# Seven-product weight sums moved from VectorE to accumulating transfers on GpSimd's queue

## The chip, the cores and the metric

The kernel runs on one core of a Trainium2 chip. The metric is the device time of one launch, in microseconds. The core has TensorE (PE, matrix products), VectorE (DVE), ScalarE (ACT), GpSimd (POOL) and SyncE (SP). In this kernel every transfer before the change is issued from SP's queue.

## The reference

A decoder of two layers on 512 tokens of 1024 features, all float32. What matters here is the MLP that ends each layer:

```
def sq_relu_mlp(h, w1, w2):
    return jnp.square(jax.nn.relu(h @ w1)) @ w2      # h 512x1024, w1 1024x4096, w2 4096x1024
```

Layer 0 has a pooling mixer ahead of its MLP, layer 1 a spatial gating unit (SGU). Each layer's norms are modulated by vectors computed from `c` and `ada_w`.

## The kernel before

**Precision.** A float32 product is made of three matmuls of float32r operands (`mm3`, lines 123 to 127): each operand is split into a high part `h` and a remainder `l`. For weights `split` (lines 113 to 118) does that: ACT copies a 128x1024 piece to `wh` (L116), then DVE makes `wl = r - wh` (L117). The pairs `wh`, `wl` lie in five buffers, so a split waits until TensorE is done with the pair five splits earlier.

**The second MLP product** takes its 4096 inner features in four chunks `c` of 1024. Chunks 0 to 2 go by a seven-product scheme on 2x2 blocks (the p units). The last chunk is done plainly in eight q units. The weights of a chunk are four blocks of 1 MB each, named b11, b12, b21, b22 and loaded by `b_of` (L400) into three buffers `b`. The activations `g` are addressed through `quad`. Some products take sums of weight blocks and sums of activations:

- products 1, 3 and 2 take b11, b22 and b21 as they are loaded;
- products 5, 6 and 4 take one tile `t` that is carried on in place: product 5 makes it b12-b11 (L416), product 6 makes it b22-t (L422), product 4 makes it t-b21 (L441);
- product 7 takes b12-b22 (L433).

So VectorE makes four weight sums of 128x2048 in each of three chunks and two layers, 24 in all. Activation sums (L418, L424, L426, L430; tiles `s` and `u`) and the split of the activations into `oh` and `ol` (L445, L446) are there too.

**Units and order.** `mlp` (line 349) lists units: f units (one 128-wide piece of the first product, 24 matmuls, then ACT's relu and square, L374 and L375), p units (24 matmuls) and q units. In one chunk the order is f f f, then p1 f p5 f p6 f p3 f p7 f p2 p4, where p5 is the unit of product 5. TensorE's order is as written. `prep` of a unit (loads, sums, splits) is written two units ahead of its matmuls. The instructions of the other engines are put into an order by a scheduler when the kernel is built, and each engine then works through its own in that order. An engine whose next instruction has to wait holds back all that stands behind it.

**Results of a p unit** are added to a tile `y` in SBUF by VectorE (L474), or copied by ACT where it is the first (L477).

**Beside it**: `ada_tile` (L143 load, L147 multiply and sum on DVE) works off the modulation vectors during the MLP. `spread_cols` (lines 154 to 162) has eight GpSimd operations (`dg`, L158) that feed four matmuls `pb` (L161), which have a fixed place in TensorE's order. GpSimd does nothing else during the MLPs.

Of the kernel before, what the change touches and what calls it, by code (L numbers as in the profile page):

```python
# [7 lines left out]
F32 = mybir.dt.float32  # L8
F32R = mybir.dt.float32r
AF = mybir.ActivationFunctionType  # L10
ALU = mybir.AluOpType
# [3 lines left out]
P = 128  # L15
D = 1024
S = 512
KD = D // P
# [30 lines left out]
def decoder_kernel(ctx: ExitStack, tc: tile.TileContext, xtok, vecs, rows, fgrow, ada0, adag, ada1, pool_w, w1s, w1, w2, w2e, w_v, w_u, w_o, wsT, lnp, bs, out):  # L49
    nc = tc.nc  # L50
    V, A, G, T = nc.vector, nc.scalar, nc.gpsimd, nc.tensor
# [18 lines left out]
    def f32(t):  # L70
        return t.bitcast(F32)

    def bank(name, pool=None):
        pool = pool or ps
        return pool.tile([P, S], F32, name=name, tag="mm" if pool is ps else "xz")
# [26 lines left out]
    def raw4(src):  # L102
        r = w4.tile([P, D], F32, name="raw", tag="w4")
        nc.sync.dma_start(r, src)
        return r
# [4 lines left out]
    def wpair():  # L110
        return wtile("wh"), wtile("wl")

    def split(r):

        h, l = wpair()
        A.activation(h, r, AF.Copy)  # L116
        V.tensor_tensor(l, r, f32(h), ALU.subtract)  # L117
        return h, l

    def cut(hl_, *ix):  # L120
        return hl_[0][ix], hl_[1][ix]

    def mm3(o, w, m, first, last, **kw):
        (wh, wl), (mh, ml) = w, m
        T.matmul(o, wl, mh, start=first, stop=False, **kw)  # L125
        T.matmul(o, wh, ml, start=False, stop=False, **kw)  # L126
        T.matmul(o, wh, mh, start=False, stop=last, **kw)  # L127
# [37 lines left out]
    def rsqrt(src, mul, eps, n):  # L165
        v = sm.tile([P, n], F32, name="rv", tag=f"rv{n}")
        V.tensor_scalar(v, src, mul, eps, ALU.mult, ALU.add)  # L167
        r = sm.tile([P, n], F32, name="rr", tag=f"rr{n}")
        G.tensor_tensor(r, v, mhalf[:, 0:n], ALU.pow)  # L169
        t = sm.tile([P, n], F32, name="rt", tag=f"rt{n}")  # L170

        V.scalar_tensor_tensor(t, v, -0.5, r, ALU.mult, ALU.mult)
        V.tensor_tensor(t, t, r, ALU.mult)
        V.scalar_tensor_tensor(r, t, 1.5, r, ALU.add, ALU.mult)
        return r


    with tc.tile_pool(name="st", bufs=1) as st, tc.tile_pool(name="st2", bufs=2) as st2:
# [12 lines left out]
        for g in range(4):  # L191
# [4 lines left out]
            for n in range(2):  # L196
                m = pm[:, n]
# [151 lines left out]
    def mlp(i, first, extra, last, ending):  # L349
# [3 lines left out]
        with (  # L353
# [23 lines left out]
            def quad(c, r, j):  # L377

                return g[c, j].rearrange("p a (h r t) -> p a h r t", h=2, r=2)[:, :, :, r]
# [13 lines left out]

            held = {}

            def b_of(c, r, n):
                t = w2p.tile([P, 4, S], F32, name="b", tag="b")
                nc.sync.dma_start(t, w2[i, c, r, n])  # L400
                return t

            def p_prep(u):
                c, m = u
                H = held

                def s_tile(name):
                    return su.tile([P, 4, 2, P], F32, name=name, tag=name)

                if m == 1:  # L410
                    wb = H["b11"] = b_of(c, 0, 0)
                    a = quad(c, 0, 0)
                elif m == 5:
                    H["b12"] = b_of(c, 0, 1)
                    wb = H["t"] = H.pop("b11")
                    V.tensor_tensor(wb, H["b12"], wb, ALU.subtract)  # L416
                    a = H["s"] = s_tile("s")
                    V.tensor_tensor(a, quad(c, 1, 0), quad(c, 1, 1), ALU.add)  # L418
                elif m == 6:
                    H["b22"] = b_of(c, 1, 1)  # L420
                    wb = H["t"]
                    V.tensor_tensor(wb, H["b22"], wb, ALU.subtract)  # L422
                    a = H["s"]
                    V.tensor_tensor(a, a, quad(c, 0, 0), ALU.subtract)  # L424
                    H["u"] = s_tile("u")
                    V.tensor_tensor(H["u"], quad(c, 0, 0), quad(c, 1, 0), ALU.subtract)  # L426
                elif m == 3:
                    wb = H["b22"]
                    a = H["s"]
                    V.tensor_tensor(a, quad(c, 0, 1), a, ALU.subtract)  # L430
                elif m == 7:
                    wb = H.pop("b12")
                    V.tensor_tensor(wb, H.pop("b22"), wb, ALU.subtract)  # L433
                    a = H.pop("u")
                    H.pop("s")
                elif m == 2:
                    wb = H["b21"] = b_of(c, 1, 0)
                    a = quad(c, 0, 1)
                else:
                    wb = H.pop("t")  # L440
                    V.tensor_tensor(wb, H.pop("b21"), wb, ALU.subtract)  # L441
                    a = quad(c, 1, 1)
                oh = op.tile([P, 4, 2, P], F32R, name="oh", tag="oh")
                ol = op.tile([P, 4, 2, P], F32R, name="ol", tag="ol")
                A.activation(oh, a, AF.Copy)  # L445
                V.tensor_tensor(ol, a, f32(oh), ALU.subtract)  # L446
                w = [split(wb[:, 2 * q : 2 * q + 2].rearrange("p a b -> p (a b)")) for q in range(2)]
                return (oh, ol), w

            X, Z = {}, {}  # L450

            TAKES = {1: (0, 0), 5: (1, 1), 6: (0, 1), 3: (0, 1), 7: (1, 1), 2: (0, 0), 4: (1, 0)}
# [3 lines left out]
            def p_run(u, ready):  # L456
                halves = (0, 1)
                c, m = u
                o, w = ready
                banks = X if m in (1, 6, 7, 4) else Z  # L460
                first, fin = m in (1, 5, 2), m in (4, 3, 2)
                if first:
                    for hf in halves:
                        banks[hf] = bank("pm", xz)
                for p in range(4):
                    wv = cut(w[p // 2], ALL, slice(S * (p % 2), S * (p % 2) + S))
                    for hf in halves:
                        mm3(banks[hf], cut(o, ALL, p, hf), wv, first and p == 0, fin and p == 3, skip_group_check=True)
                for hf in halves:
                    r, dh = TAKES[m]  # L470
                    t = 2 * hf + r
                    yt = y[:, t, S * dh : S * dh + S]
                    if (t, dh) in seen:
                        V.tensor_tensor(yt, yt, banks[hf], ALU.add)  # L474
                    else:
                        seen.add((t, dh))
                        A.activation(yt, banks[hf], AF.Copy)  # L477
                    if c == 2 and LAST.get(m) == (r, dh):

                        V.tensor_tensor(yt, yt, gb[:, S * dh : S * dh + S], ALU.mult)  # L480
                        V.tensor_tensor(x[:, t, S * dh : S * dh + S], x[:, t, S * dh : S * dh + S], yt, ALU.add)
# [4 lines left out]
            def q_prep(u):  # L486
                dh, t = u
                if t == 0:
                    wq[dh] = [split(raw4(w2e[i, dh, q].rearrange("p a b -> p (a b)"))) for q in range(4)]
                if dh:  # L490
                    return kept[t]
                if t < 2:
                    oh = op.tile([P, KD, P], F32R, name="qh", tag="oh")
                    ol = op.tile([P, KD, P], F32R, name="ql", tag="ol")
                else:
                    o = w2p.tile([P, 2, KD, P], F32R, name="qo", tag="b")
                    oh, ol = o[:, 0], o[:, 1]
                for j in range(2):
                    a, k = g[3, j][:, :, tok[t]], slice(4 * j, 4 * j + 4)
                    A.activation(oh[:, k], a, AF.Copy)  # L500
                    V.tensor_tensor(ol[:, k], a, f32(oh[:, k]), ALU.subtract)
                kept[t] = oh, ol
                return kept[t]
# [14 lines left out]
            for c in range(3):  # L518
# [3 lines left out]
                for m in (1, 5, 6, 3, 7, 2, 4):  # L522
                    units.append(("p", (c, m)))
                    if fs:
                        units.append(fs.pop(0))
            units += [("q", (dh, t)) for dh in range(2) for t in range(NT)]
            prep = {"f": f_prep, "p": p_prep, "q": q_prep}
            run = {"f": f_run, "p": p_run, "q": q_run}
            ready = {}
            extra = list(extra)  # L530
# [57 lines left out]
    ex += [lambda: spread_cols(mods[0][:, c_g(1, 0) : c_g(1, 0) + KD])]  # L588
    ex += [lambda q=q: ada_tile(1, q, ada1[8 + q], get4) for q in range(24)]
    mlp(0, first0, ex, gated, lambda: normed(0, 1, 0))  # L590


# [6 lines left out]
    with (  # L599
# [8 lines left out]
        wb = vp.tile([P, 2, HEADS, P], F32, name="wsbs")  # L608
# [18 lines left out]
        for t in range(NT):  # L627
# [6 lines left out]
            r = rsqrt(ag[:, 1:2], 1.0, LN_EPS, 1)  # L634
# [73 lines left out]
    def last1(t, dh, yt):  # L708
        gated(t, dh, yt)
        if dh == 1:  # L710
            r = rms(t)
            for n in range(2):
                c = slice(S * n, S * n + S)
                V.scalar_tensor_tensor(x[:, t, c], x[:, t, c], r, fgb[0][:, c], ALU.mult, ALU.mult)
                nc.sync.dma_start(out[t, :, n], x[:, t, c])

    mlp(1, first1, ex, last1, lambda: None)


# [74 lines left out]
```

## Time and profile before

| | |
|---|---|
| time, median of 3 runs | 920.51 us (920.27 to 920.9) |
| the profiled execution's own time | 922.86 us |
| its span, first to last instruction | 921.1 us |
| PE busy | 96% of the span |
| DVE busy | 653.6 us, 71% |
| ACT busy | 418.3 us, 45% |
| POOL busy | 46.0 us, 5% |
| HBM read | 135.87 MB |
| transfers from SP's queue | 42.9% of 16 DMA engines' span |

The first MLP's units lie at about 121 to 410 us, the SGU at 410 to 562 us, the second MLP at 562 to 921 us. A busy TensorE is not one at its peak, because a matmul's modelled end overlaps the next one's start; so a stage is also read by the distance from one matmul's start to the next. A group's line reads: line, engine, operation, output <- inputs, count | busy us, mean ns of one | idle time of the engine just before, and what ended it.

### The profile page before, as it was taken

To read this page: it belongs to the slowest core of one execution; us is meant where nothing else is said; L and a number is where in the kernel's file an instruction comes from. 1 tells how busy PE (TensorE), PEld (TensorE's weight loads), DVE (VectorE), ACT (ScalarE), POOL (GpSimd) and SP (SyncE) were. 2 spreads that over 40 slices of the span, in tenths; PEclk is the share of its full clock that TensorE was granted. 3 is DMA by queue.
4 is the path that set the end of the run, shared out by engine and by line. 5 is a ranking of instruction groups with operands and counts; after the bars stand their busy time and mean duration, and the time that the engine had idled before them with its cause. 6 is when DMAs were issued, how large, how long until landed. Compare 5 with 4: busy or idle time off the path is not lost.

```text
span 921.1 us, 10624 instructions
## 1 busy us (share of the span) xinstructions
PE 884.2 (96%) x4054; PEld 729.7 (79%) x4054; DVE 653.6 (71%) x910; ACT 418.3 (45%) x592; POOL 46.0 (5%) x98
## 2 busy tenths in 40 slices
PE   5987999999999999999998898999999999999996
PEld 3975888788888888888877687988887888888875
DVE  3678787678888888757587836267677576667945
ACT  7262365554444455347222426265545445445421
POOL 5000002000000000000200000000004000000000
PEclk9997999999999999999999999999999999999998
DMA  9946762554455351513357504452443134112212
GB/s 359 409 142 224 268 246 92 182 191 152 155 188 176 122 181 49 204 67 138 116 171 240 183 23 158 162 184 69 158 139 122 39 122 168 54 51 87 92 46 92
DMA packets 35045, 138.67 MB, mean 151 GB/s; under 512 B 3889, under 2 KB 4017, under 8 KB 31665
## 3 DMA queue, kind: packets, MB, share of 16 engines
q1 hardware_dynamic: 34994, 137.99, 42.9%
q8 instruction: 32, 0.52, 0.2%
q14 instruction: 19, 0.16, 0.1%
HBM read 135.87 MB, written 2.10 MB: 150 GB/s over the span
## 4 chain that ended last, share of the span: by engine, by line
PE 83%; DVE 7%; DMA 4%; ACT 3%; issue 2%; POOL 1%; DVEq 0%; SPq 0%; POOLq 0%; ACTq 0%
PE po L125 15%; PE po L126 15%; PE po L127 15%; PE pm L126 11%; PE pm L127 11%; PE pm L125 11%; PE pg L263 2%; DVE wl L117 2%; DMA ada<-in_ada 1%; DVE ada L147 1%; ACT wh L116 1%; DMA raw<-in_w_u 1%; PE po L292 1%; PE pq L252 1%; DVE v L637 1%
## 5 line engine op out<-in xcount | busy, mean ns | idle before, releaser
L125 PE MATMUL po<-hh,wl 128*128 128x512 f32 (+1 forms) x608 | 233.8, 384 | 9.2 <-DVE wl L117 6.7
L126 PE MATMUL po<-hl,wh 128*128 128x512 f32 (+1 forms) x608 | 231.4, 381 | 0.9 <-DVE hl L329 0.9
L127 PE MATMUL po<-hh,wh 128*128 128x512 f32 (+1 forms) x608 | 231.2, 380 | 0.0
L117 DVE TENSOR_TENSOR wl<-raw,wh 128x1024 fp32r<-128x1024 f32 x97 | 118.4, 1222 | 53.4 <-ACT wh L116 53.3
L117 DVE TENSOR_TENSOR wl<-b,wh 128x1024 fp32r<-128x1024 f32 x84 | 102.5, 1221 | 68.2 <-ACT wh L116 68.2
L125 PEld LDWEIGHTS po<-hh,wl 128*128 128x128 f32 x608 | 115.7, 190 | 34.3 <-DVE wl L117 8.4
L116 ACT ACTIVATE wh<-raw 128x1024 fp32r<-128x1024 f32 x97 | 102.4, 1058 | 84.9 <-PE pm L127 33.8
L126 PEld LDWEIGHTS po<-hl,wh 128*128 128x128 f32 x608 | 115.7, 190 | 23.4 <-DVE hl L329 1.4
L127 PEld LDWEIGHTS po<-hh,wh 128*128 128x128 f32 x608 | 115.5, 190 | 21.4
L127 PE MATMUL pm<-wh,oh 128*128 128x512 f32 x336 | 130.7, 389 | 0.0
L125 PE MATMUL pm<-wh,ol 128*128 128x512 f32 x336 | 130.7, 389 | 0.0
L126 PE MATMUL pm<-wl,oh 128*128 128x512 f32 x336 | 130.7, 389 | 0.0
L374 ACT ACTIVATE g<-po 128x512 f32<-128x512 f32 x64 | 37.8, 599 | 165.3 <-PE po L127 165.3
L147 DVE SCALAR_TENSOR_TENSOR ada<-ada,cb 128x1024 f32<-128x1024 f32 x66 | 80.2, 1218 | 22.2 <-DMA ada<-in_ada 22.0
L116 ACT ACTIVATE wh<-b 128x1024 fp32r<-128x1024 f32 x84 | 88.4, 1052 | 15.2 <-PE pm L127 10.1
L126 PEld LDWEIGHTS pm<-wl,oh 128*128 128x128 f32 x336 | 63.0, 188 | 13.1
L127 PEld LDWEIGHTS pm<-wh,oh 128*128 128x128 f32 x336 | 63.1, 188 | 13.1
L125 PEld LDWEIGHTS pm<-wh,ol 128*128 128x128 f32 x336 | 63.1, 188 | 13.1
L551 ACT ACTIVATE tmp<-x 128x512 f32<-128x512 f32 x24 | 15.1, 630 | 71.5 <-DVE x L548 71.5
L474 DVE TENSOR_TENSOR y<-y,pm 128x512 f32<-128x512 f32 x68 | 43.4, 679 | 0.0
L375 ACT ACTIVATE g<-g 128x512 f32<-128x512 f32 x64 | 39.5, 627 | 0.0
L169 POOL TENSOR_TENSOR rr<-rv,mhalf 128x1 f32<-128x1 f32 (+1 forms) x18 | 12.8, 711 | 423.8 <-DVE rv L167 412.5
(145 smaller groups left out, 1145.0 us busy)
## 6 DMA issues: line engine op xcount, KB each, us to landing
ada<-in_ada SPq DMA_DIRECT2D x66, 512.0 KB, 4.2
raw<-in_w SPq DMA_DIRECT2D x57, 512.0 KB, 3.3
b<-in_w SPq DMA_DIRECT2D x24, 1024.0 KB, 4.8
raw<-in_w2e SPq DMA_DIRECT2D x16, 512.0 KB, 3.4
wh<-in_ada SPq DMA_DIRECT2D x11, 512.0 KB, 7.0
wl<-in_ada SPq DMA_DIRECT2D x11, 512.0 KB, 10.0
raw<-in_w_v SPq DMA_DIRECT2D x8, 512.0 KB, 3.8
raw<-in_w_u SPq DMA_DIRECT2D x8, 512.0 KB, 4.2
```

The source lines that it names most:

```text
L116: A.activation(h, r, AF.Copy)
L117: V.tensor_tensor(l, r, f32(h), ALU.subtract)
L125: T.matmul(o, wl, mh, start=first, stop=False, **kw)
L126: T.matmul(o, wh, ml, start=False, stop=False, **kw)
L127: T.matmul(o, wh, mh, start=False, stop=last, **kw)
L147: V.scalar_tensor_tensor(r, r, 1.0, cb, ALU.mult, ALU.mult, accum_out=pmv[i, b][:, j : j + 1])
L169: G.tensor_tensor(r, v, mhalf[:, 0:n], ALU.pow)
L263: T.matmul(o, cab[:, k], r[:, k], start=(k == 0), stop=False)
L374: A.activation(t, po, AF.Relu)
L375: A.activation(t, t, AF.Square)
L474: V.tensor_tensor(yt, yt, banks[hf], ALU.add)
L551: A.activation(tmp, x[:, t, c], AF.Square, accum_out=sums[t][:, dh : dh + 1])
```

## The change

The seven products are written in another form, in which all weight sums are additions: `t` is b11 for product 1, b11+b12 for product 5, b11+b12+b22 for product 6 and b11+b12+b22+b21 for product 4; product 7 takes b12+b22. The signs move to an activation sum (product 5 subtracts, product 3 adds) and to the results of products 6 and 7, which are subtracted from `y` or copied with a scale of -1.

The additions are made by transfers that read a weight block from HBM and add it to the tile in SBUF (`accum_op`), issued from GpSimd's queue as soon as the splits that read the tile's old contents are done. `t` has a tile of its own, `bt` with one buffer; `b` has two buffers in place of three. 24 DVE operations go; 24 transfers of 1 MB come. The plain loads stay 24.

```
 def b_of(c, r, n):
-    t = w2p.tile([P, 4, S], F32, name="b", tag="b")
+    t = w2p.tile([P, 4, S], F32, name="b", tag="b", bufs=2)
...
 if m == 1:
-    wb = H["b11"] = b_of(c, 0, 0)
+    wb = H["t"] = w2p.tile([P, 4, S], F32, name="bt", tag="bt", bufs=1)
+    nc.sync.dma_start(wb, w2[i, c, 0, 0])
 elif m == 5:
-    H["b12"] = b_of(c, 0, 1)
-    wb = H["t"] = H.pop("b11")
-    V.tensor_tensor(wb, H["b12"], wb, ALU.subtract)
+    wb = H["t"]
-    V.tensor_tensor(a, quad(c, 1, 0), quad(c, 1, 1), ALU.add)
+    V.tensor_tensor(a, quad(c, 1, 0), quad(c, 1, 1), ALU.subtract)
 elif m == 6:
-    H["b22"] = b_of(c, 1, 1)
     wb = H["t"]
-    V.tensor_tensor(wb, H["b22"], wb, ALU.subtract)
...
 elif m == 3:
-    wb = H["b22"]
-    V.tensor_tensor(a, quad(c, 0, 1), a, ALU.subtract)
+    wb = b_of(c, 1, 1)
+    H["b12"] = b_of(c, 0, 1)
+    V.tensor_tensor(a, quad(c, 0, 1), a, ALU.add)
 elif m == 7:
     wb = H.pop("b12")
-    V.tensor_tensor(wb, H.pop("b22"), wb, ALU.subtract)
 elif m == 2:
-    wb = H["b21"] = b_of(c, 1, 0)
+    wb = b_of(c, 1, 0)
 else:
     wb = H.pop("t")
-    V.tensor_tensor(wb, H.pop("b21"), wb, ALU.subtract)
...
 w = [split(wb[:, 2 * q : 2 * q + 2].rearrange("p a b -> p (a b)")) for q in range(2)]
+if m in NEXT:
+    G.dma_start(wb, w2[i, c, NEXT[m][0], NEXT[m][1]], accum_op=ALU.add)
+if m == 3:
+    G.dma_start(H["b12"], w2[i, c, 1, 1], accum_op=ALU.add)
...
+NEXT = {1: (0, 1), 5: (1, 1), 6: (1, 0)}
...
+minus = m in (6, 7)
-        V.tensor_tensor(yt, yt, banks[hf], ALU.add)
+        V.tensor_tensor(yt, yt, banks[hf], ALU.subtract if minus else ALU.add)
-        A.activation(yt, banks[hf], AF.Copy)
+        A.activation(yt, banks[hf], AF.Copy, scale=-1.0 if minus else 1.0)
```

More of the change, by code (lines that the diff above doesn't have):

```diff
@@ L427, in p_prep @@
                 elif m == 3:
-                    wb = H["b22"]
-                    a = H["s"]
-                    V.tensor_tensor(a, quad(c, 0, 1), a, ALU.subtract)
+                    wb = b_of(c, 1, 1)
+                    H["b12"] = b_of(c, 0, 1)
+                    a = H.pop("s")
+                    V.tensor_tensor(a, quad(c, 0, 1), a, ALU.add)
                 elif m == 7:
                     wb = H.pop("b12")
-                    V.tensor_tensor(wb, H.pop("b22"), wb, ALU.subtract)
                     a = H.pop("u")
-                    H.pop("s")
                 elif m == 2:
-                    wb = H["b21"] = b_of(c, 1, 0)
+                    wb = b_of(c, 1, 0)
                     a = quad(c, 0, 1)
@@ L468, in p_run @@
                         mm3(banks[hf], cut(o, ALL, p, hf), wv, first and p == 0, fin and p == 3, skip_group_check=True)
+                r, dh = TAKES[m]
+                minus = m in (6, 7)
                 for hf in halves:
-                    r, dh = TAKES[m]
                     t = 2 * hf + r
@@ L495, in q_prep @@
                 else:
-                    o = w2p.tile([P, 2, KD, P], F32R, name="qo", tag="b")
+                    o = w2p.tile([P, 2, KD, P], F32R, name="qo", tag="b", bufs=2)
                     oh, ol = o[:, 0], o[:, 1]
```

## The prediction

> **What bounds the kernel now.** I read the page's table of engines first, then busy time by stage, then who waited for whom, and last the order in time around one chunk.
>
> ```profile
> PE 884.2 (96%) x4054; PEld 729.7 (79%) x4054; DVE 653.6 (71%) x910; ACT 418.3 (45%) x592; POOL 46.0 (5%) x98
> ```
>
> Busy time by stage (columns: stretch, its length, then busy us of PE, PEld, DVE, ACT, POOL, granted clock, DMA share, GB/s); 121 to 366 is the first MLP's f and p units, 605 to 860 the second's:
>
> ```profile
> 121.00:366.00 245.00, 245.00 (x1079) 202.17 (x1078) 200.19 (x230) 123.48 (x154) 6.46 (x8) 1.00 0.45 152
> 562.00:605.00 43.00, 39.85 (x272) 36.87 (x271) 21.80 (x40) 23.14 (x38) 1.10 (x2) 0.96 0.46 171
> 605.00:860.00 255.00, 255.00 (x1122) 210.38 (x1123) 178.44 (x172) 126.61 (x159) 9.72 (x8) 1.00 0.31 108
> ```
>
> In both stretches that hold the changed work TensorE is never idle. Since a busy PE can hide slow issue, I checked the distance from one matmul's start to the next in the chain of waits there: 0.227 us, matmul after matmul, at clock 1.00. So a unit of 24 matmuls takes 5.44 us, and ScalarE's relu of successive f units starts at that distance too (212.68, 218.12, 223.56). VectorE is busy 82% (200.19 of 245) and 70% (178.44 of 255): it follows, it does not lead. PE's waits from 562 us on, which are for VectorE (total, times, longest):
>
> ```profile
> PE po L125 <- DVE wl L117: 3.1, 3, 1.7
> PE pm L126 <- DVE wl L117: 0.2, 1, 0.2
> ```
>
> The 3.1 us lie ahead of 605, in the start of the second MLP, where no weight sum stands. What the change frees is time of an engine on which TensorE does not wait.
>
> **The change part by part.** *Removed:* 24 sums on VectorE (groups by line; count, busy us, mean ns, idle before):
>
> ```profile
> L422 DVE TENSOR_TENSOR b<-b 128x2048 f32<-128x2048 f32 x6 | 13.7, 2287 | 0.1
> L416 DVE TENSOR_TENSOR b<-b 128x2048 f32<-128x2048 f32 x6 | 13.7, 2284 | 0.0
> L441 DVE TENSOR_TENSOR b<-b 128x2048 f32<-128x2048 f32 x6 | 13.7, 2283 | 0.0
> L433 DVE TENSOR_TENSOR b<-b 128x2048 f32<-128x2048 f32 x6 | 13.7, 2281 | 0.0
> ```
>
> 4 x 13.7 = 54.8 us of VectorE. All of it lies beside matmuls at full pace, so its worth in the span is 0. At most the two waits above could go, 3.3 us, if work of VectorE were pulled ahead; I take 0.
>
> *Kept:* signs change at no cost: the same operations on the same shapes. In the built order of the changed kernel TensorE, ScalarE and SP have the same operations in the same order as before (on SP some loads go to `bt`); VectorE's order lacks the 24 sums and is otherwise shuffled a little; GpSimd's has 24 transfers more, so the change does what it says.
>
> *Added:* 24 transfers of 1 MB that read HBM and add into SBUF. What they cost depends on one length: X, from the VectorE split that frees the tile to the landing of the sum. The trace has no such transfer and none from GpSimd's queue. Nearest rows, of plain 1 MB loads, the page's DMA part (count, KB, median us to landing) and the answer for tile `b`:
>
> ```profile
> b<-in_w SPq DMA_DIRECT2D x24, 1024.0 KB, 4.8
> ```
>
> ```profile
> DMA to landing us min/median/max: 4.6/4.8/8.1
> ```
>
> Below, X is at least a plain load's 4.6 us. Above, the slowest row is pool_w's 1 MB at the start, 11.7 us with the DMA engines at 0.77 share; if the add makes the bytes pass twice, 23.4 us. I take two median loads, 2 x 4.8 = 9.6 us, since the load of this very array is the nearest row and an add needs two operands fetched.
>
> The Trainium skill (Collectives: The Full Stack, The bandwidth ceiling) says that a transfer that adds has no cost for the add but needs two source reads, so that it ran at half the rate of a copy, about 31 GB/s per engine. By it 16 engines would need some 4.2 us for 1 MB, an estimate from that page, and X would be shorter than mine; no run here shows it yet, and the sum would be the same.
>
> *Is X hidden?* Tile `t` is a chain: split for p1, add, split for p5, add, split for p6. Chunk 1 of the first MLP, from the time order of VectorE and ScalarE (start, length, engine, line):
>
> ```profile
> 210.35 1.22 DVE L117 TENSOR_TENSOR wl<-b,wh 128x1024 fp32r<-128x1024 f32 x1
> ...
> 225.14 1.23 DVE L117 TENSOR_TENSOR wl<-b,wh 128x1024 fp32r<-128x1024 f32 x1 [2.20 <-ACT wh L116]
> ```
>
> ```profile
> 218.62 1.06 ACT L116 ACTIVATE wh<-b 128x1024 fp32r<-128x1024 f32 x1
> ...
> 224.06 1.05 ACT L116 ACTIVATE wh<-b 128x1024 fp32r<-128x1024 f32 x1
> ...
> 232.08 1.06 ACT L116 ACTIVATE wh<-b 128x1024 fp32r<-128x1024 f32 x1 [2.01 <-DVE b L422]
> ```
>
> ```profile
> 245.12 0.39 PE L125 MATMUL pm<-wh,ol 128*128 128x512 f32 x1
> ```
>
> p1's second split ends at 210.35 + 1.22 = 211.57; p5's are at 218.62 and 224.06 on ScalarE and end on VectorE at 226.4; p6's first is at 232.08; p6 starts on TensorE at 245.12. With X = 9.6 the first add lands at 221.2. ScalarE waits 2.6 us at 218.62, and the rest of p5's splits still ends about 226. The second add lands at 236.0, p6's split is done 1.05 + 1.23 us later, at 238.3: 6.8 us to spare. The third add (for p4, split at 269.8) and product 7's (b12 loaded from 188, used at 251.7) have over 15 us to spare.
>
> If X is longer, the chain moves as a whole: X, then 4.2 us (two wh of p5, two half-tile operations of ScalarE between them, one wl: 0.95 + 0.5 + 0.5 + 1.05 + 1.23), X again, then 2.3 us. It is late when 2X + 6.5 exceeds the time from p1's split to p6's start. That time, from the same rows of the six chunks, is 34.3, 33.55, 35.6, 35.1, 36.8 and 35.6 us. So the first chunk is late from X = 13.5 us, all from 15.2, and then the price is the sum of the six, 12X - 171 us, since p6 has to wait in TensorE's fixed order.
>
> *What is held up behind a waiting instruction:* on ScalarE the relu of an f unit and the next raw split. The latter is done some 10 us before use (split for f4 ends at 228.6, f4 starts at 239.4). On GpSimd, `dg` of the second MLP now stands behind an add; it ended at 704.9 and its matmuls `pb` started at 708.5, 3.6 us to spare; the add's tile is loaded by about 690, before `dg` could begin (695). On SP the `bt` load waits for p4's split just as a `b` load did (269.91 to 276.3). 24 MB more are read: four adds of two passes at the page's best rate, 409 GB/s, are 20.5 us of all engines per chunk of 81.8 us, so the DMA share would rise from 0.45 to about 0.70. That stays below the 0.77 of the start, and raw loads have 9 us of lead over a median landing of 3.3.
>
> **Sum:** 0 gained, 0 lost. The profiled execution took 922.86 us, 1.76 more than its span of 921.1 and 2.35 more than the median of the three runs. The same in the changed kernel gives a median of **920.5 us**.
>
> **Rivals.**
> - *The adds are late* (slower): place p6 in each chunk, price 2 us per us of X and chunk, deciding from X = 13.5. With two slowest plain landings, 2 x 8.1 = 16.2, 12 x 16.2 - 171 = 23 us: 943. At 23.4 us it is 110: 1030. For it: nothing shows how fast a transfer adds, and it now shares engines with raw and ada loads. Against: the median row leaves 3.9 us per add. Chance 0.26.
> - *GpSimd writes its transfers slowly beside a busy VectorE* (slightly slower). GpSimd's operations are stretched beside other work:
>
> ```profile
> L158 POOL TENSOR_SCALAR dg<-ident,mods x24: 597/602/2672, 156.2 to 704.3; 128x128 f32<-128x128 f32 x24
> ```
>
>   602 ns is the median; the longest, 2672, is in the stretch 695 to 705, where VectorE was busy 7.40 of 10 us (2.57 of 7 at 156 to 163, longest there 2389). If one add had to wait out four VectorE operations of 1.22 us, X would be 9.6 + 4.9 = 14.5 and the three shortest chunks would lose 1.2, 2.0 and 0.4 us: 924. The Trainium skill (SBUF — State Buffer, the box on "DVE blocks DMA") has such a rule: a transfer from GpSimd's queue is stalled while VectorE runs an operation that locks the shared port; but its part Who interferes with whom finds that for copies and not for tensor_tensor, which is nearly all of VectorE's work here, so I keep the chance small. Chance 0.13.
> - *VectorE's free time shortens a start-up* (faster): up to 3.3 us of waits, 918. Against: they stand where no sum was removed. Chance 0.07.
>
> Forecast 0.54. A change under 0.2% (1.84 us) can hardly be told from none. So faster 0.07, same 0.54, slower 0.39. The range runs from 918 to 945, which leaves out about half of the late-add rival and little else, some 0.13; the likeliest case alone is 918.7 to 922.3.
>
> **What would show it.** Right: VectorE near 600 us, TensorE without a wait between 121 and 366 and between 605 and 860, start distance 0.227 us, X below 13.5 us. Wrong: waits of ScalarE's `wh<-bt` for transfers that exceed 10 us, followed by waits of PE `pm` for `wl` ahead of p6; or `pb` waiting for `dg`. The forecast fails if X is over 13.5 us, or if plain loads land later than their 9 us of lead.

## The result and the profile after

The changed kernel takes **931.08 us** (median of 4 runs, 929.4 to 934.34), the kernel before 920.7 us beside it (median of 4, 920.27 to 921.37): a ratio of 1.0116, 95% interval 1.0088 to 1.0145, so it is **slower by 1.2%**. The profiled execution took 930.9 us with a span of 929.2 us, 8.1 us more than the span before, at nearly the same mean clock (0.988 against 0.986).

The page's table of engines, of the changed kernel:

```profile
PE 884.1 (95%) x4054; PEld 727.2 (78%) x4054; DVE 601.1 (65%) x886; ACT 415.2 (45%) x592; POOL 71.8 (8%) x122
```

VectorE lost 52.5 us of work (653.6 to 601.1), TensorE has as much as before, and the span grew: TensorE idles more. Where, is told by the busy time by stage (columns as above: stretch, length, then PE, PEld, DVE, ACT, POOL, granted clock, DMA share, GB/s):

```profile
121.00:366.00 245.00, 236.78 (x1033) 193.06 (x1032) 161.79 (x202) 112.46 (x143) 21.60 (x20) 1.00 0.69 201
562.00:605.00 43.00, 39.92 (x265) 36.73 (x264) 22.11 (x47) 20.03 (x31) 2.59 (x4) 0.96 0.57 195
605.00:860.00 255.00, 254.92 (x1130) 210.45 (x1129) 148.48 (x153) 128.28 (x163) 19.40 (x19) 1.00 0.55 153
```

All of the loss is in the first MLP, 8.2 us of TensorE idle in 245. The second, with the same twelve adding transfers, keeps TensorE busy for 254.92 of 255. The next stage confirms it: GpSimd's first operation of the norm between the MLP and the gating unit starts at 409.96 us in place of 400.63, 9.3 later. That is the 8.2 us, and 0.16 us for each of the seven waits listed below: idle time is counted from the modelled end of a matmul, 0.39 us after its start, where the next would have started after 0.227.

Who waited for whom between 121 and 366 us (total, times, longest):

```profile
DVE ada L147 <- DMA ada<-in_ada: 72.7, 23, 11.1
ACT wh L116 <- DMA bt<-in_w: 58.1, 7, 15.1
...
PE pm L126 <- DVE wl L117: 3.5, 4, 1.3
PE po L125 <- DVE wl L117: 3.2, 2, 2.0
PE pm L125 <- ACT wh L116: 1.5, 1, 1.5
```

The same query on the kernel before:

```profile
DVE ada L147 <- DMA ada<-in_ada: 5.3, 6, 1.7
```

Read this from the bottom. TensorE's three rows add up to 8.2 us, all of the idle time. They are waits for splits. ScalarE's splits wait for `bt`, the tile into which the transfers add. The first row shown is in no account of the change: VectorE's wait for its **ada** loads went from 5.3 to 72.7 us, though nothing in the diff touches them.

The DMA part gives the lengths (count, KB, median us to landing):

```profile
ada<-in_ada SPq DMA_DIRECT2D x66, 512.0 KB, 5.5
bt<-in_w POOLq DMA_DIRECT2D x18, 1024.0 KB, 8.7
b<-in_w POOLq DMA_DIRECT2D x6, 1024.0 KB, 10.7
```

An add into `bt` lands 8.7 us after its issue, so X is near the 9.6 us of the prediction. Half a megabyte of ada, within the first MLP alone, before and after (two answers on the tile `ada`):

```profile
DMA to landing us min/median/max: 3.1/3.5/5.5
```

```profile
DMA to landing us min/median/max: 3.1/6.1/12.1
```

How the two meet is seen in chunk 0, in the order in time of GpSimd, ScalarE, VectorE and TensorE of the changed kernel:

```profile
127.37 1.06 POOL L450 DMA_DIRECT2D bt<-in_w  x1 [59.69 <-DVE wl L117]
128.16 1.18 POOL L452 DMA_DIRECT2D b<-in_w  x1
151.84 0.86 POOL L450 DMA_DIRECT2D bt<-in_w  x1 [22.49 <-DVE wl L117]
```

```profile
135.52 1.06 ACT L116 ACTIVATE wh<-bt 128x1024 fp32r<-128x1024 f32 x1 [1.57 <-DMA bt<-in_w]
139.28 1.05 ACT L116 ACTIVATE wh<-bt 128x1024 fp32r<-128x1024 f32 x1
...
160.90 1.06 ACT L116 ACTIVATE wh<-bt 128x1024 fp32r<-128x1024 f32 x1 [15.12 <-DMA bt<-in_w]
```

```profile
144.67 1.23 DVE L147 SCALAR_TENSOR_TENSOR ada<-ada,cb 128x1024 f32<-128x1024 f32 x1 [11.05 <-DMA ada<-in_ada]
...
145.82 1.22 DVE L117 TENSOR_TENSOR wl<-bt,wh 128x1024 fp32r<-128x1024 f32 x1
...
149.18 1.23 DVE L147 SCALAR_TENSOR_TENSOR ada<-ada,cb 128x1024 f32<-128x1024 f32 x1 [2.06 <-DMA ada<-in_ada]
...
150.33 1.22 DVE L117 TENSOR_TENSOR wl<-bt,wh 128x1024 fp32r<-128x1024 f32 x1
```

```profile
162.01 0.49 PE L125 MATMUL pm<-wh,ol 128*128 128x512 f32 x1 [1.50 <-ACT wh L116]
```

The first add is issued at 127.37 and has landed at 135.52, when ScalarE starts p5's split on it. ScalarE is done with both halves at 140.33. VectorE's part of the split, though, comes at 145.82 and 150.33: VectorE takes its work in a fixed order, and ahead of it stand two multiplies on ada tiles. The first of these tiles was issued at 132.51, while the adds into `bt` and `b` (127.37 and 128.16) were in flight, and lands 12.1 us later. VectorE does nothing for 11.05 us with a split behind it whose input has been there since 136.6. So the second add leaves at 151.84, lands at 160.9, and p6 starts 1.5 us late. From the first add's landing to the second's issue it took 16.3 us, where the prediction had 4.2.

### The profile page after: what moved, and what is told of

Its sections match the earlier page's. It is cut to its first block, busy times and chain, and to the rows that moved or that the text cites. A ratio compares the mean times of both kernels' runs of the same rounds, so it can differ in the third digit from the quotient of the medians.

```text
span 929.2 us, 10693 instructions
## 1 busy us (share of the span) xinstructions
PE 884.1 (95%) x4054; PEld 727.2 (78%) x4054; DVE 601.1 (65%) x886; ACT 415.2 (45%) x592; POOL 71.8 (8%) x122
## 3 DMA queue, kind: packets, MB, share of 16 engines
q0 software_dynamic: 3456, 25.17, 14.7%
## 4 chain that ended last, share of the span: by engine, by line
PE 60%; DMA 20%; DVE 11%; issue 4%; ACT 3%; POOL 1%; DVEq 0%; SPq 0%; POOLq 0%; ACTq 0%
DMA ada<-in_ada 15%; PE po L125 10%; PE po L126 10%; PE po L127 10%; PE pm L126 8%; PE pm L127 8%; PE pm L125 8%; DVE wl L117 4%; DVE ada L147 2%; PE pg L263 2%; ACT wh L116 1%; DMA wh<-in_ada 1%; PE po L292 1%; DMA bt<-in_w 1%; DMA raw<-in_w_u 1%
## 5 line engine op out<-in xcount | busy, mean ns | idle before, releaser
L117 DVE TENSOR_TENSOR wl<-bt,wh 128x1024 fp32r<-128x1024 f32 x48 | 58.4, 1223 | 47.2 <-ACT wh L116 47.2
L116 ACT ACTIVATE wh<-bt 128x1024 fp32r<-128x1024 f32 x48 | 50.5, 1055 | 80.7 <-DMA bt<-in_w 75.7
L117 DVE TENSOR_TENSOR wl<-b,wh 128x1024 fp32r<-128x1024 f32 x36 | 43.9, 1221 | 16.5 <-ACT wh L116 16.4
L450 POOL DMA_DIRECT2D bt<-in_w x18 | 15.9, 886 | 329.8 <-DVE wl L117 317.7
```

Source lines behind the costliest of these rows:

```text
L450: G.dma_start(wb, w2[i, c, NEXT[m][0], NEXT[m][1]], accum_op=ALU.add)
```

## The experiments

Theory A: ada loads land late beside adding transfers, and VectorE, which takes them in its order, passes their lateness to the splits behind them. Theory B, the rival: two adding transfers in a row are by themselves too long for the time from p1's split to p6's start. All were run in five rounds beside the kernel before, whose median was 921.52, 921.07 and 920.94 us in the three groups (experiments 1 to 4, 5 to 8, 9 to 12). Experiments 6 and 11 edit the kernel before, the others the changed kernel.

**1. The new form with its sums on VectorE.** Of the change, the signs alone.

```
-wb = H["t"]
+H["b12"] = b_of(c, 0, 1)
+wb = H["t"] = H.pop("b11")
+V.tensor_tensor(wb, H["b12"], wb, ALU.add)
...
-if m in NEXT:
-    G.dma_start(wb, w2[i, c, NEXT[m][0], NEXT[m][1]], accum_op=ALU.add)
```

> The changed kernel's form of the seven products (all weight sums additions, signs in an activation sum and in the results) with the 24 sums made by VectorE again and three b buffers, no transfer that adds. Both theories put the loss on the transfers and give the time before: 920.7 us, within 0.2%. If the signs or the order of products cost something, it shows here: then up to 931.

Measured 921.66 us, ratio 1.0001 (0.9992 to 1.0011); TensorE busy 245 of 245 us. The form costs nothing; the transfers are the cause.

**2 and 3. Adding transfers in one MLP only**: `add = i == 1` in the second, `add = i == 0` in the first, with the other MLP as in experiment 1.

> Adding transfers in the second MLP only, VectorE's sums (in the new form) in the first. Theory A (loads of ada tiles land late beside the adding transfers, and VectorE, which waits for them in its order, holds back the splits; ada tiles are many in the first MLP only) gives the time before, 920.7 us within 0.2%. Theory B (two adding transfers one after the other are by themselves too long for the time between p1's split and p6) gives about half of the loss, 925 to 926, since three of the six chunks are here.

> Adding transfers in the first MLP only. Theory A gives the whole loss, 929 to 932 us. Theory B gives half of it, 925 to 926.

In the second MLP alone: 921.24 us, ratio 0.9998 (0.999 to 1.0007), with an add landing in 8.7 us all the same. In the first alone: 937.6 us, ratio 1.0178 (1.0154 to 1.0201), VectorE's wait for ada there 75.1 us. So an add of this length is hidden where few ada tiles stand (8 in the second MLP, 32 in the first), and the first MLP holds all of the loss. That experiment 3 lost more than the whole change was not expected; experiments 9 and 10 return to it.

**4. The same transfers as plain copies.** Without `accum_op`, the sums are left out; queue, size, order and waits stay.

```
-G.dma_start(wb, w2[i, c, NEXT[m][0], NEXT[m][1]], accum_op=ALU.add)
+G.dma_start(wb, w2[i, c, NEXT[m][0], NEXT[m][1]])
```

> As the changed kernel, but the 24 transfers from GpSimd's queue are plain copies that overwrite the tile (the weight sums are left out). If an adding transfer passes its bytes twice, a plain one takes about half of the DMA engines' time (queue share 7% to 8% in place of 14.7%) and lands in 5 to 6 us in place of 8.6. Theory A: ada loads land sooner, VectorE waits for them less than half as long in the first MLP (under 35 us in place of 72.7), the time is 921 to 924. Theory B: the chain is 2 x 3 us shorter per chunk, the waits of p6 go, the time is 921 to 923 too; the two differ in whether VectorE's wait for ada goes with it.

Measured 921.51 us, ratio 0.9999 (0.999 to 1.0008). The DMA rows of the page, first the changed kernel's queue of adds, then this one's (packets, MB, share of 16 engines; then count, KB, us to landing):

```profile
q0 software_dynamic: 3456, 25.17, 14.7%
```

```profile
q0 software_dynamic: 3456, 25.17, 7.7%
...
bt<-in_w POOLq DMA_DIRECT2D x18, 1024.0 KB, 5.1
```

The same packets and bytes take the engines 14.7 x 929.2 / (7.7 x 919.8) = 1.9 times as long as an add. As copies they land in 5.1 us and ada in 4.4 (6.1 beside adds), and VectorE's wait for ada is 36.4 us in 22 waits of at most 3.5: a little over the 35 that theory A had set, and too short to matter. The two `b` buffers and the tile `bt` are as in the changed kernel. So it is the add, with its longer time on the DMA engines, that hurts, and not the buffers, GpSimd's queue or its waits. Both theories expect that.

**5 and 6. The changed kernel, and the kernel before, without the 32 ada tiles of the first MLP** (what they compute is filled with a constant).

```
-ex = [lambda q=q: ada_tile(0, 40 + q, ada1[q], get4) for q in range(8)]
+ex = [lambda: None for q in range(8)]
```

> The changed kernel without the 32 ada tiles of the first MLP (neither loaded nor multiplied; the modulation vectors that they give are filled with 0.5). Theory A: no wait is left for TensorE in the first MLP, the same time as the kernel before without these tiles, within 0.2%. Theory B: p6 still waits in the first MLP, 3 to 5 us more than that kernel.

> The kernel before without the 32 ada tiles of the first MLP (neither loaded nor multiplied; the modulation vectors that they give are filled with 0.5). TensorE was never idle there, so both theories give the time before or very little less: 919 to 921 us. It is the base for the changed kernel without these tiles.

Measured 921.36 us, ratio 1.0002 (0.9993 to 1.0011), and 921.17 us, 0.9998 (0.9986 to 1.0009). The adds still land in 8.6 us, and TensorE has no wait left. **Theory B falls**: two adds in a row fit into the time that they have.

**7. The 32 ada multiplies kept, their loads left out**: VectorE multiplies the tile `cb` in place of a loaded one.

> The changed kernel with the 32 ada tiles of the first MLP multiplied but not loaded: VectorE has the same operations, on the tile cb in place of a loaded one (so the modulation vectors differ). Theory A (the late landing is what holds VectorE back): no wait is left, 920 to 922 us. If it is VectorE's work on ada, or its new order, and not the landing: 928 to 931. Theory B: p6 still waits, 923 to 926.

Measured 920.73 us, ratio 0.9992 (0.998 to 1.0003). It is not VectorE's time on the ada tiles but the wait for their loads. Nor did the other transfers land sooner for want of the ada loads: the adds into `bt` take 8.4 us and the raw loads 4.6, against 8.7 and 4.3 in the changed kernel.

**8. Each add into `t` cut into two of 512 KB**, each issued when its own half has been split.

```
-G.dma_start(wb, w2[i, c, NEXT[m][0], NEXT[m][1]], accum_op=ALU.add)
+for q in range(2):
+    G.dma_start(wb[:, 2 * q : 2 * q + 2],
+                w2[i, c, NEXT[m][0], NEXT[m][1]][:, 2 * q : 2 * q + 2], accum_op=ALU.add)
```

> The changed kernel with each adding transfer into t cut into two halves of 512 KB, each issued when its own half has been split; the same bytes. Theory B: the chain from p1's split to p6 is some 4 to 8 us shorter per chunk, the waits of p6 (4.4 of the 8.2 us) go, 925 to 927 us or less. Theory A: the bytes and the landing of ada tiles are as before, so VectorE is still held back; the waits of f units (3.3 us) and part of p6's stay, 927 to 931.

Measured 920.99 us, ratio 0.9996 (0.9985 to 1.0008). **Theory A's expectation missed**: the late ada loads are all there, and yet the loss is gone, with the waits of the f units that A expected to stay. (B's "or less" was met, though experiment 5 rules B out.) The waits from 121 to 366 us, and the same place of chunk 0, on VectorE, ScalarE and TensorE:

```profile
DVE ada L147 <- DMA ada<-in_ada: 66.3, 24, 11.2
ACT wh L116 <- DMA bt<-in_w: 41.2, 10, 6.3
```

```profile
144.20 1.23 DVE L147 SCALAR_TENSOR_TENSOR ada<-ada,cb 128x1024 f32<-128x1024 f32 x1 [11.20 <-DMA ada<-in_ada]
...
145.35 1.22 DVE L117 TENSOR_TENSOR wl<-bt,wh 128x1024 fp32r<-128x1024 f32 x1
```

```profile
152.55 1.06 ACT L116 ACTIVATE wh<-bt 128x1024 fp32r<-128x1024 f32 x1 [6.17 <-DMA bt<-in_w]
...
160.36 1.07 ACT L116 ACTIVATE wh<-bt 128x1024 fp32r<-128x1024 f32 x1 [6.27 <-DMA bt<-in_w]
```

```profile
160.95 0.39 PE L125 MATMUL pm<-wh,ol 128*128 128x512 f32 x1
```

VectorE stands still for ada as long as in the changed kernel (11.20 us, until 144.20). But the first half's add no longer waits for the second half's split, is there at 152.55, and p6, which begins on that half, starts at 160.95 without a wait. So the loss needs both: a late ada load ahead of p5's splits, and a chain whose every link waits for the whole tile. Take away either (5 and 7 the one, 8 the other) and it is gone. One thing beside the cut differs in number 8: VectorE's order as built has p6's first split ahead of an ada multiply in chunks 1 and 2 (in chunk 1 at 236.78, the multiply at 241.25), where the changed kernel has both splits behind it (the multiply at 245.96, the splits at 247.11). What the cut and the order each gave there was not told apart; in chunk 0 no ada multiply stands between p5's splits and p6's first one in either.

**9 and 10. The changed kernel and experiment 3 once more, side by side**, unedited.

> The changed kernel as it is, beside the next run, to learn whether the larger loss with adds in the first MLP alone (937.6 against 931.1 us) belongs to that kernel or to the occasion. If to the occasion, this and the next one give medians within 2 us of each other; if to the kernel, this gives 929 to 934 and the next one 934 to 941 again. In both cases all idle time of TensorE in the two MLPs lies in the first one: TensorE busy 234 to 238 of 245 us between 121 and 366 us, VectorE's wait for ada loads there 65 to 80 us.

> Adding transfers in the first MLP alone, sums of the second on VectorE. Occasion: within 2 us of the changed kernel of the same call. Kernel: 934 to 941 us, 4 us and more above it.

Measured 935.35 us, ratio 1.0168 (1.015 to 1.0186), and 934.16 us, 1.0144 (1.013 to 1.0158): 1.2 us apart. The larger loss of experiment 3 belonged to the occasion and not to the kernel. TensorE is busy 236.31 of 245 us in number 9, as expected, and 239.10 in number 10, more than the 238 expected; VectorE waits for ada 71.3 and 73.4 us. So neither TensorE's idle time nor the lateness of ada tells why these runs are slower than those of the first comparison: number 10 idles 2.3 us less there than the changed kernel's first profile, and its profiled execution took 3.2 us more (934.07 against 930.9). What differs is the granted clock. Two stretches of number 9, each at the start of a p6 (columns as above, the clock behind POOL):

```profile
163.23:170.06 6.83, 6.23 (x15) 4.94 (x16) 6.78 (x9) 6.83 (x10) 3.43 (x2) 0.50 0.49 113
337.31:340.72 3.41, 3.05 (x7) 2.47 (x8) 2.41 (x3) 3.41 (x5) 0.88 (x1) 0.50 0.49 154
```

At half clock the matmuls start 0.427 us apart in place of 0.227, so these 10.2 us lose some 4.8 (an estimate: 10.2 x (1 - 0.227/0.427)); number 9's profiled execution was 4.1 us slower than the first. Number 10 has 10.2 us of the same, at the starts of two p6, and experiment 3 has 6.8. The first profile has none: there the clock is 1.00 at the same place, behind waits of 1.50 and 0.76 us against 1.58 and 0.76 in number 9. What decides whether the clock drops behind such a wait stays open. The loss is 1.2 to 1.8% over these four comparisons. Kernels without the loss do not vary so (experiments 1, 2 and 4 to 8 lie within 1 us of each other), and none of their profiles has such a stretch in the first MLP.

**11 and 12. What VectorE's freed time is worth.** If VectorE has time to spare in the first MLP, it can take over the 16 ada tiles of the gating unit, whose loads head 9.6 us of VectorE's idle time between 440 and 526 us while TensorE idles 5.5. Number 11 moves them in the kernel before, with all its sums on VectorE; number 12 in the kernel of experiment 8.

```
-ex += [lambda q=q: ada_tile(1, q, ada1[8 + q], get4) for q in range(24)]
+ex += [lambda q=q: ada_tile(1, q, ada1[8 + q], get4) for q in range(40)]
...
-    ex += [lambda q=q: ada_tile(1, q, ada1[8 + q], get4) for q in range(24, 40)]
```

> The kernel before with the 16 ada tiles of the gating unit (440 to 526 us, where TensorE idles 5.5 of 86 us and VectorE is busy 68) moved into the first MLP, which then has 48 of them; no adding transfers. VectorE in 121 to 366 us goes from 200.2 to about 200.2 + 16 x 1.22 = 219.7 of 245 us. If what holds up TensorE in the gating unit is VectorE's order with its ada loads (they head 9.6 us of its idle time there), 3 to 5 us are gained: 916 to 918. If it is something else in the gating unit, 920.5 to 921.5. If the first MLP has no room for 16 more tiles, over 922.

> The same move of 16 ada tiles on top of the changed kernel with its adds into t cut into halves. VectorE in 121 to 366 us about 172.5 + 19.5 = 192 of 245 us. If VectorE's time is what the first MLP lacks for more ada tiles, this is the faster of the two moves (916 to 918). If it is the late ada loads beside adding transfers and the slack of the chain, as the runs so far say, 48 tiles in place of 32 bring the idle time of TensorE back, and this is slower than the move without adding transfers, by 2 to 10 us (920 to 928).

Number 11 measured **913.9 us, ratio 0.9922 (0.991 to 0.9935)**, faster than both kernels and than expected; number 12 938.02 us, 1.0187 (1.0169 to 1.0205), worse than the 920 to 928 expected. Busy time by stage, 11 and then 12:

```profile
121.00:366.00 245.00, 244.54 (x1075) 201.48 (x1075) 217.43 (x271) 125.52 (x158) 13.34 (x8) 1.00 0.53 183
440.00:526.00 86.00, 85.78 (x407) 71.00 (x406) 50.92 (x78) 27.20 (x38) 8.36 (x12) 1.00 0.27 86
```

```profile
121.00:366.00 245.00, 230.10 (x998) 186.20 (x997) 167.02 (x225) 110.07 (x140) 28.54 (x29) 1.00 0.78 225
440.00:526.00 86.00, 86.00 (x404) 71.18 (x403) 54.62 (x88) 36.26 (x50) 9.18 (x13) 1.00 0.32 105
```

In 11 VectorE is busy 217.43 of 245 us, 89%, and TensorE still waits for no more than 0.5 us: its time there was never scarce. The gating unit's idle time shrinks from 5.5 to 0.2 us, which is 5.3 of the 7.0 us gained; another 1.7 us or so (half of 3.41) show in the granted clock, which in the kernel before is 0.50 from 526.08 to 529.49 us and in number 11 is 1.00 from 440 to 566. Whether that comes of the move was not tested. In 12 VectorE is busy 50 us less in the first MLP, the DMA share is 0.78 in place of 0.53, and TensorE loses 14.9 us. The resource that this kernel can spare is VectorE; what the change spends is lead of its loads.

## Why the prediction was wrong

- *TensorE bounds both MLPs and VectorE's sums are worth 0*: right. VectorE went to 601 us as forecast, and experiment 11 shows it from the other side: 17 us more of VectorE in the same stage cost nothing.
- *The signs cost nothing*: right (experiment 1).
- *X = 9.6 us*: right within a tenth. In chunk 0 it is 8.7 us from the end of p1's split (126.77) to the landing (135.52), and the landings' median is 8.7 from issue. The estimate of 4.2 us for 1 MB from the rate in the Trainium skill (Collectives: The Full Stack, The bandwidth ceiling) was too short by half. The Trainium skill has that rate from a ring's reduce step, where an add needs two source reads and runs at half the rate of a copy. The trace agrees with the ratio, 1.9 times the engine time of a copy, and shows nothing of the reads.
- *DMA share 0.45 to about 0.70*: right, 0.69.
- *"raw loads have 9 us of lead over a median landing of 3.3"*: **this step failed, by what it leaves out.** For raw loads it nearly held: between 121 and 366 us they land in 3.3 us in the median and 11.2 at most, and one was waited for, 2.4 us. But the account of *what is held up behind a waiting instruction* named ScalarE, GpSimd and SP, and of the loads only the raw ones. VectorE was left out, since it only lost work. But VectorE's order holds 32 multiplies on ada tiles, whose loads get one of three buffers (shared with raw loads) only when VectorE frees one, and so have next to no lead: already before it waited for 6 of them, 5.3 us in all. At a share of 0.69 they land in up to 12.1 us, splits stand behind them, and the wait became 72.7 us. The late-add rival names ada loads, but as what delays an add and not as what an add delays.
- *"4.2 us" of engine work between the two adds*: failed in consequence. It was taken as the sum of the operations; it was 16.3 us in chunk 0. The sum 2X + 6.5 = 25.7 us had 7.9 us and more to spare in every chunk, and one late load of 11 us, with the next behind it, took it. With the measured lengths chunk 0 needs 8.7 + 16.3 + 9.1 + 1.1 = 35.2 us from the end of p1's split at 126.77, and p6 was due at 160.35, 33.6 us after it.
- *The price*: TensorE's waits ahead of p6 are 1.50 + 0.76, 1.27 and 0.87 us, 4.4 in all. The other 3.8 us are ahead of two f units (1.28 and 1.96) and of a p3 (0.57), whose splits stood behind ada tiles in VectorE's order. They are not apart from the chain: experiment 8 shortens the chain, leaves the ada loads late, and has none of these waits. The six times sum to 210.95 us, so the rival's price is 12X - 172 and not 171; nothing hangs on it.
- *Rivals*: "the adds are late" named the place (p6) and the signs (`wh<-bt` over 10 us, then PE `pm` waiting for `wl`), and both came. Its condition, X over 13.5 us, was not met: the chain was late by its start, not by the transfer. GpSimd's issue of an add took 0.86 to 1.18 us, and the adds into `bt` in the two MLP stretches landed in at most 9.6 us, so nothing shows a part of that rival. (Its "nearly all of VectorE's work" was too much: by the trace's groups tensor_tensor is 533 of 696 us before, scalar_tensor_tensor 135.)

The second MLP holds the same transfers, the same X and the same chain but few ada tiles, and loses nothing. That was the comparison to make ahead of the run: the two stages differ in what else stands in VectorE's order.

## What to carry to other kernels

When a change adds DMA traffic, list every load that is used during it, with its lead over its landing, and start with the one that is waited for already, however shortly: the engine that heads those waits delays everything in its order, even when it has less to do than before. A chain of transfer, split, transfer is as long as the worst wait in the order of each engine in it; cutting the tile so that a half can go ahead took back the whole loss here, though not with 16 more late loads (experiment 12). And time freed on an engine that follows is worth nothing until other work is put there; here that could be done without freeing any.

## What the runs showed of the hardware

- A transfer that reads 1 MB from HBM and adds it into SBUF lands 8.7 us after its issue (median), a plain one on the same queue in 5.1; it takes 1.9 times the DMA engines' time.
- Of two adds issued 0.8 us apart, the one into `bt` at 127.37 landed in 8.1 us, the one into `b` at 128.16 in 15.5. A plain 512 KB load issued 4 us after them on SP's queue landed in 12.1 us, against 3.5 in the median before. The Trainium skill (DMA: Bandwidth & Descriptors, Issuing engines are not separate DMA queues) says that transfers of all issuing engines run on the same 16 DMA engines and interleave; the traces agree, and give the price.
- In experiments 3, 9 and 10 TensorE's granted clock was 0.50 for 3.4 or 6.8 us at the start of a p6 that had been waited for, with matmuls 0.427 us apart in place of 0.227. In the changed kernel's first profile such waits (1.50 and 0.76 us) left it at 1.00. So a wait of TensorE can cost more than its length, and not each time.
